# Rotary turn of the differential queries and keys: from GpSimd to VectorE and transfers issued by SyncE

## Chip, cores and metric

The kernel runs on one core of a Trainium2 chip. The metric is the device time of one execution in microseconds; a profiled execution gives the rows below. TensorE multiplies matrices, VectorE and ScalarE work on elements, GpSimd does the rest, and SyncE issues the transfers. The profile calls them PE (with PEld for its weight loads), DVE, ACT, POOL and SP.

## What is computed

Two transformer blocks of two layers each, one sequence of 256 tokens, 1024 features, fp32. The change touches the second block. A layer of it projects the input x into three branches and merges them:

```python
z, xbc, dt_raw, dq, dk, dv, dg, cq, cg, gl = jnp.split(proj, splits, axis=-1)
y_ssd = _ssd_branch(z, xbc, ...)      # scan over tokens; then y * silu(z), rms norm
q = _apply_rope(dq, cos, sin)         # each head: 2 x 64 features
k = _apply_rope(dk, cos, sin)
...                                   # differential attention over q, k, v, then norm
y_cross = ...                         # attention to a memory
merged = g0 * (y_ssd @ w0) + g1 * (y_diff @ w1) + g2 * (y_cross @ w2)

def _apply_rope(t, cos, sin):
    t1, t2 = t[..., :32], t[..., 32:]
    return concat([t1 * c - t2 * s, t1 * s + t2 * c])
```

With features on the partitions the turn is `t * cosT + swapped(t) * sinT`, where `swapped` exchanges the 32-row halves of every 64 partitions and the sign lies in `sinT`. [...]

## The kernel before

A product of 256 tokens with 256 output features is a "gemm" (`gemm`, line 320): two pieces of 24 matmuls each, into one PSUM bank `g`. For each piece the weights `w` arrive in 512 KB transfers (L280, up to 8 pieces ahead) and are split in two parts, `wh` by ScalarE (L290) and `wl` by VectorE (L292), up to 4 pieces ahead. Pieces wait in a queue `e.q`; `fill(n)` runs n of them between steps of other work, `need(tag)` runs the queue until no piece of that tag is left. A scheduler then sets the order of instructions on every engine from the order of the code, with the splits given priority.

In a layer of the second block the scan goes over 32 heads, two at a time. For each head (`scan_a`) GpSimd spreads a row over the partitions (L1456, PARTITION_BROADCAST into `E`) and cuts it twice (L1460, AFFINE_SELECT), ScalarE takes six exponentials (L1455), VectorE adds and multiplies (L1463, L1464). `scan_b` then multiplies the pair's `E` with the inputs (`yps`) and adds the result into `xsT` (L1476). `E` has four buffers. Between heads `fill` runs 48 pieces, and 48 are queued when the scan begins: the last 16 are those of `dq` and `dk`, four gemms each.

At the end of each of these eight gemms ScalarE copies the bank into `dq` or `dk` (L1418). After every second one `rotate` turns 128x1024 on GpSimd: four transfers issued by GpSimd into `sw` (L1404, L1405), then three operations (L1408 to L1410). Behind the scan come the eight `z` gemms (VectorE multiplies into `xsT`, `split` gives `ysh` and `ysl`), the gate and product of the state space branch (`b0`, 24 pieces), and between their pieces the differential attention `diff`, head by head, which begins with the products `ds` of `dq` and `dk`.

Of the kernel before, what the change touches and what calls it, by code (L numbers as in the profile page):

```python
# [16 lines left out]
P = 128  # L17
S = 256
# [6 lines left out]
# ------------------------------------------------------------------ host layout  # L25
# small parameters and constants that are loaded together: name, columns
# [8 lines left out]
# Column groups (256 wide) of the first block's w_in.  # L35
# [15 lines left out]
def _chunks(v, n=P):  # L51
    """[..., C] -> [n, ..., C / n] (feature on the partition)."""
    v = np.asarray(v)
    lead = v.shape[:-1]
    r = v.reshape(lead + (v.shape[-1] // n, n))
    return np.ascontiguousarray(np.moveaxis(r, -1, 0)).reshape(n, -1)


def _pack_in(w):
    """[L, K, G * 256] -> [L, G, 128, K / 128 * 256]: 256 output columns at a time."""  # L60
    L, K, M = w.shape
    r = w.reshape(L, K // P, P, M // 256, 256).transpose(0, 3, 2, 1, 4)
    return np.ascontiguousarray(r).reshape(L, M // 256, P, -1)


def _pack_rows(w):
    """[L, G * 256, 1024] -> [L, G, 128, 2 * 1024]: 256 contraction rows at a time."""
    L, K, M = w.shape
    r = w.reshape(L, K // 256, 2, P, M).transpose(0, 1, 3, 2, 4)
    return np.ascontiguousarray(r).reshape(L, K // 256, P, -1)  # L70
# [8 lines left out]
def _constants():  # L79
# [5 lines left out]
    dist = (t[:, None] - t[None, :]).astype(np.float32)  # [q, k]  # L85
# [16 lines left out]
    # compressed branch: bias and mask, [128, 2 (q tile), 4, 16]  # L102
# [7 lines left out]
    # rotary tables of the latent mixer: rows 64..95 of a head  # L110
# [14 lines left out]
    # second block: frequencies  # L125
# [8 lines left out]
def _pack(inp):  # L134
# [4 lines left out]
    # [L, 6 (modulation), 4, 128, 2 * 1024]: 256 contraction rows at a time  # L139
# [8 lines left out]
    # [L, 4, 128, 2 * 1024]: twice half of the contraction, two groups of 256 columns; twice a quarter, all groups  # L148
# [20 lines left out]
    # second block  # L169
# [35 lines left out]
# ------------------------------------------------------------------ device  # L205
NW, NS = 8, 4  # buffers of the streamed weights: raw, split
AHEAD_W, AHEAD_S = 8, 4  # pieces fetched, split ahead
SPLIT_FIRST, NORM_FIRST = 100, 200  # steps by which splits and norms go ahead in the schedule
NU = 11  # units of [128, 2048] words
# [6 lines left out]
class Emit:  # L216
# [50 lines left out]
    # ---- streamed weights, in the order of their use and in pieces of 1024 columns: the raw  # L267
    # tile, then its rounded part and the remainder
# [35 lines left out]
    # ---- queue of matrix products that fill the tensor engine's waits  # L304
# [15 lines left out]
    def gemm(self, tag, keys, act, evac, tok=False, half=None):  # L320
        """Queue a product of 256 tokens and 256 output features (the contraction in steps of
        1024, one key each; with half, half of a step); act(i) gives the two parts of the
        activations of step i. Features on the partitions, or tokens (tok)."""
# [37 lines left out]
    def token_sum(self, st, c, p, first, last):  # L361
        """st[token, tile] += sum over the partitions of c [p, 256]"""
# [3 lines left out]
    def spread(self, col):  # L366
        """[128 tokens, 2] -> PSUM [128, 256], the same on all partitions"""
# [19 lines left out]
    def fold(self, pool, box, pair):  # L387
        """box[0] += a pair of chunks [128, 512]"""
# [7 lines left out]
    def fold_sum(self, box):  # L396
        """the sums over features, [token, tile]"""
# [28 lines left out]
# ------------------------------------------------------------------ memory keys and values  # L426
# [9 lines left out]
def mem_gemm(e, l, g, hl, mk, mv, tag="mem"):  # L436
    """Group g of the layer's memory keys (0..3, features on the partitions) and values (4..7)."""
# [7 lines left out]
# ------------------------------------------------------------------ first block  # L445
def block1(e, ctx, mem0):
# [7 lines left out]
    # order of the streamed weights  # L454
    ada = lambda l, s: [("w_ada", l, s, n) for n in range(4)] if l < DEPTH else []
    zorder = (0, 1, 2, 3, 5, 4, 6, 7, 8)
    # modulations (shift, scale, gate; twice a layer) in the mixers, at the second norm, in the
    # products after it and at the next layer's norm
# [6 lines left out]
    MEM = 6  # memory groups at the start; the others come after the block  # L465
# [19 lines left out]
    # silu(c), replicated over 32 columns  # L485
# [13 lines left out]
    def ada_step(l, s, n):  # L499
        """a step of one of the layer's modulations: four column blocks side by side"""  # L500
# [21 lines left out]
    def ada_pool(l, s, n):  # L522
        """the same step on GpSimd: weighted rows, still to be summed over the partitions"""
# [31 lines left out]
    # the first modulations arrive at the memory's pace: its keys and values go between  # L555
# [29 lines left out]
    class Attend:  # L585
        """q(h), k(h): [d, 256] on partitions; v(h, t): [128, 64]; o: two PSUM tiles."""
# [4 lines left out]
        def scores(self):  # L591
            q, k, bs, par = self.q, self.k, self.bs, self.par
            # heads whose keys lie on different row tiles go to different banks
# [75 lines left out]
    def mixers(l, ah, al, oh, ol, ev_x):  # L669
# [70 lines left out]
        # compressed keys and values  # L740
# [5 lines left out]
        def compress(i):  # L746
# [5 lines left out]
            # element (lp, b) is token 16 b + 2 lp (+ 1 on the upper half)  # L752
# [33 lines left out]
        # latent attention: norms, queries, keys, values  # L786
# [27 lines left out]
        # rotary part, rows 64..95  # L814
# [20 lines left out]
        # gates of the sparse mixer  # L835
# [7 lines left out]
        # sliding window: heads 0, 2 | 1, 3 share a chunk of queries  # L843
# [16 lines left out]
        # sparse mixer: compressed, selected and window branches into one output  # L860
# [73 lines left out]
    for l in range(DEPTH):  # L934
# [40 lines left out]
        def down(g):  # L975
            """two pieces; the last one finishes one pair of chunks after the other"""
# [68 lines left out]
# ------------------------------------------------------------------ second block  # L1045
def block2(e, ctx, xh, xl, mk, mv, out):
# [18 lines left out]
    # halves, so that silu(u) = (tanh(u / 2) + 1) * (u / 2)  # L1065
# [5 lines left out]
    # rotary tables from the positions: reduced to [-pi, pi]  # L1071
# [36 lines left out]
    def silu2(ps_, dst):  # L1108
        """dst = 2 silu(ps_)"""
# [4 lines left out]
    # order of the streamed weights  # L1114
# [21 lines left out]
    def soft(scs, scale):  # L1136
        """scs: PSUM [128, 2, 256] -> exponentials, reciprocals of their sums [128, 2]"""
# [10 lines left out]
    def turn(src, dst, eng):  # L1148
        """src: [128 q, 2 (tile), 256 k] -> dst [128 k, 2 (tile), 256 q]"""
# [6 lines left out]
    def finish(l, xh, xl, act, G):  # L1156
        """the last product and layer norm, with the tokens on the partitions"""
# [33 lines left out]
        # the last groups one half of the tokens after the other  # L1191
# [14 lines left out]
    for l in range(DEPTH):  # L1206
# [17 lines left out]
        # ---------------- memory cross attention  # L1224
        def conv(ps, ch, dst):
            """channels ch, ch + 1 (128 each)"""
# [12 lines left out]
        bcT = v3(e.unit("bcT"), 8)  # B of the four groups, then C  # L1239
# [44 lines left out]
        # step sizes, [64 (direction, head), 256]  # L1284
# [7 lines left out]
        LO = e.t(cp, [P, S], "LO")  # rows 0..63: running sums in a chunk; 64..127: rest of the chunk  # L1292
        Lc = e.t(cp, [64, S], "Lc")  # the running sums alone
        bias = e.t(cp, [P, 2, P], "ltok")  # per token: log of the step and minus the running sum, or rest of the chunk

        def steps():
# [26 lines left out]
            # log of the step sizes, added to the exponents  # L1323
# [28 lines left out]
        # ---------------- queue of what the scan leaves room for  # L1352
# [49 lines left out]
        def rotate(tq, sw, hs):  # L1402
            for p0 in range(0, P, 64):
                nc.gpsimd.dma_start(sw[p0 : p0 + 32, hs, :], tq[p0 + 32 : p0 + 64, hs, :])  # L1404
                nc.gpsimd.dma_start(sw[p0 + 32 : p0 + 64, hs, :], tq[p0 : p0 + 32, hs, :])  # L1405
            sb_ = sinT.unsqueeze(1).to_broadcast([P, 4, S])
            cb_ = cosT.unsqueeze(1).to_broadcast([P, 4, S])
            nc.gpsimd.tensor_tensor(sw[:, hs, :], sw[:, hs, :], sb_, ALU.mult)  # L1408
            nc.gpsimd.tensor_tensor(tq[:, hs, :], tq[:, hs, :], cb_, ALU.mult)
            nc.gpsimd.tensor_tensor(tq[:, hs, :], tq[:, hs, :], sw[:, hs, :], ALU.add)  # L1410

        for key in ("dq", "dk"):
            for g in range(4):
                def ev_d(ps, g=g, key=key):
                    if g == 0:
                        dqk[key] = v3(e.unit(key), KC)
                        dqk["sw"] = v3(e.unit("sw"), KC)
                    nc.scalar.copy(dqk[key][:, 2 * g : 2 * g + 2, :], v3(ps, 2))  # L1418
                    if g % 2 == 1:
                        rotate(dqk[key], dqk["sw"], slice(4 * (g // 2), 4 * (g // 2) + 4))  # L1420
                e.gemm("dqk", G(key, g), act, ev_d)

        # ---------------- scan, one head at a time; two heads share a chunk of features
        state = {}

        def scan_a(h):
            g = h // 8
            if h % 8 == 0:
                e.need(f"xs{g}")
                if g % 2 == 0:  # L1430
                    state["xst"] = e.unit("xst")  # [token, (group, tile, channel)]
# [15 lines left out]
            # running sums of both directions on all partitions: [source chunk, token], then the other direction  # L1447
            # inside a chunk; GpSimd copies them and cuts off what the direction does not reach
# [18 lines left out]
        def scan_b(h, Es, xst):  # L1467
            """the pair of heads h, h + 1"""
# [8 lines left out]

        pend, Es = None, []
        for h in range(32):
            E, xst = scan_a(h)  # L1480
            Es.append(E)
            if pend:
                scan_b(*pend)
                pend = None
# [3 lines left out]
        scan_b(*pend)  # L1488
        e.need("dqk")

        # ---------------- gate of the state space branch, its norm
        ysh = [v3(e.unit("ysh", F32R), KC) for _ in range(2)]
        ysl = [v3(e.unit("ysl", F32R), KC) for _ in range(2)]
        stb, rsb = [], []
        for g in range(8):
            def ev_z(ps, g=g):
# [170 lines left out]
```

## Time and profile before

| | us |
|---|---|
| three runs | 1917.38, 1905.91, 1910.5 (median 1910.5) |
| span of the profiled execution | 1906.2 |
| PE busy in it | 1805.6 (95%) |
| DVE busy | 1339.7 (70%) |
| ACT busy | 1015.5 (53%) |
| POOL busy | 427.1 (22%) |

The profiled execution is given by its span alone; that span lies 4.3 us below the median of the runs and 0.3 us above the lowest. A busy share is an average over stages: what a stage is worth is read from its own stretch.

### The profile page before, as it was taken

The page shows a single profiled execution, that of the slowest core. Times are in us where ns is not written, and L with a number is a line of the kernel's source. Part 1 is how long each engine was busy: PE and PEld are TensorE (multiplying, and loading weights), DVE is VectorE, ACT ScalarE, POOL GpSimd, SP SyncE. Part 2 cuts the span into 40 slices and gives each one's busy share as a digit, 9 for nine tenths or more (in the row PEclk, how much of TensorE's full clock was granted, in tenths as well). Part 3 has the DMA queues.
Part 4 walks back from the last instruction along what each step waited for, and adds up shares of the span by engine and source line. Part 5 has one row for each costly group of instructions (what it writes and reads, how often), then busy time and mean ns, then how long its engine had stood idle before and what let it go on. Part 6 is the DMA issues. An engine that isn't in the chain of part 4 may idle for free.

```text
span 1906.2 us, 37110 instructions
## 1 busy us (share of the span) xinstructions
PE 1805.6 (95%) x14800; PEld 1703.3 (89%) x14800; DVE 1339.7 (70%) x2164; ACT 1015.5 (53%) x1882; POOL 427.1 (22%) x347
## 2 busy tenths in 40 slices
PE   7999999999989999999997699999999999499998
PEld 6878899978879999999996599999999998399998
DVE  4576766756778556887973897667787884597566
ACT  3454444434554445567874375454556774365542
POOL 0000463600028000013543601100002543601100
PEclk9999999999989999999999799999999999799999
DMA  9873876776357555443443353455543444245451
GB/s 333 320 262 128 296 250 207 243 274 221 129 204 256 179 188 182 167 147 138 155 164 103 122 175 135 174 203 177 181 166 136 135 164 144 88 162 181 145 177 67
DMA packets 96685, 346.86 MB, mean 182 GB/s; under 512 B 11776, under 2 KB 12928, under 8 KB 96256
## 3 DMA queue, kind: packets, MB, share of 16 engines
q1 hardware_dynamic: 94976, 340.30, 51.0%
q0 software_dynamic: 1536, 4.20, 0.8%
q8 instruction: 116, 1.90, 0.4%
q14 instruction: 57, 0.47, 0.1%
HBM read 339.01 MB, written 1.05 MB: 178 GB/s over the span
## 4 chain that ended last, share of the span: by engine, by line
PE 83%; DVE 6%; ACT 3%; issue 3%; DMA 2%; POOL 2%; POOLq 0%; SPq 0%; DVEq 0%; ACTq 0%
PE g L318 62%; PE acc L318 9%; DVE wl L292 2%; PE yps L318 1%; ACT wh L290 1%; PE ada L318 1%; PE sc L318 1%; PE o L318 1%; ACT E L1455 1%; DMA w<-w_mem 1%; PE do L318 1%; PE ds L318 1%; PE xo L318 1%; PE xs L318 1%; PE tw L1153 1%
## 5 line engine op out<-in xcount | busy, mean ns | idle before, releaser
L292 DVE TENSOR_TENSOR wl<-w,wh 128x1024 fp32r<-128x1024 f32 x518 | 686.3, 1329 | 358.0 <-ACT wh L290 356.4
L290 ACT CAST wh<-w 128x1024 fp32r<-128x1024 f32 x518 | 540.5, 1048 | 511.6 <-PE g L318 327.6
L318 PE MATMUL g<-xh,wh 128*128 128x256 f32 x1664 | 477.7, 287 | 3.3 <-ACT wh L290 2.7
L318 PE MATMUL g<-xh,wl 128*128 128x256 f32 x1664 | 473.2, 284 | 3.0 <-DVE wl L292 3.0
L318 PE MATMUL g<-xl,wh 128*128 128x256 f32 x1664 | 473.8, 285 | 0.0
L318 PEld LDWEIGHTS g<-xh,wh 128*128 128x128 f32 x1664 | 320.7, 193 | 15.9 <-issue 5.9
L318 PEld LDWEIGHTS g<-xh,wl 128*128 128x128 f32 x1664 | 321.0, 193 | 4.0 <-DVE wl L292 3.8
L318 PEld LDWEIGHTS g<-xl,wh 128*128 128x128 f32 x1664 | 321.1, 193 | 2.1 <-issue 2.0
L318 PE MATMUL g<-ah,wh 128*128 128x256 f32 x736 | 210.7, 289 | 3.1 <-ACT ah L552 3.1
L318 PE MATMUL g<-al,wh 128*128 128x256 f32 x736 | 211.0, 287 | 1.5 <-DVE al L553 1.5
L318 PE MATMUL g<-ah,wl 128*128 128x256 f32 x736 | 211.3, 288 | 0.7 <-DVE wl L292 0.7
L358 POOL TENSOR_TENSOR rsy<-rv,mhalf 128x2 f32<-128x2 f32 (+1 forms) x14 | 13.4, 957 | 882.2 <-DVE rv L375 778.1
L1455 ACT ACTIVATE E<-E,ltok 128x128 f32<-128x128 f32 x384 | 123.8, 395 | 116.1 <-POOL E L1456 65.7
L318 PE MATMUL acc<-pt,wh 128*128 128x256 f32 x1024 | 183.4, 280 | 1.0 <-DVE pt L971 1.0
L1456 POOL PARTITION_BROADCAST E<-rows x64 | 92.3, 1502 | 383.6 <-PE tw L1153 157.8
L318 PEld LDWEIGHTS acc<-pt,wh 128*128 128x128 f32 x1024 | 156.9, 188 | 1.6 <-DVE pt L971 1.2
L318 PEld LDWEIGHTS g<-ah,wh 128*128 128x128 f32 x736 | 142.5, 195 | 6.8 <-issue 3.5
L318 PEld LDWEIGHTS g<-al,wh 128*128 128x128 f32 x736 | 143.3, 195 | 3.4 <-DVE al L553 2.8
L318 PEld LDWEIGHTS g<-ah,wl 128*128 128x128 f32 x736 | 143.1, 194 | 1.3 <-DVE wl L292 1.1
L318 PE MATMUL acc<-pt,wl 128*128 128x256 f32 x512 | 142.3, 279 | 0.0
L531 POOL TENSOR_SCALAR sb<-w,ca 128x1024 f32<-128x1024 f32 x24 | 92.0, 3834 | 62.4 <-PE ada L318 32.8
L318 PEld LDWEIGHTS acc<-pt,wl 128*128 128x128 f32 x512 | 96.2, 188 | 0.0
(389 smaller groups left out, 3630.2 us busy)
## 6 DMA issues: line engine op xcount, KB each, us to landing
w<-w_ada SPq DMA_DIRECT2D x96, 512.0 KB
w<-w_up SPq DMA_DIRECT2D x64, 512.0 KB
w<-w_down SPq DMA_DIRECT2D x64, 512.0 KB
w<-w_br SPq DMA_DIRECT2D x64, 512.0 KB
w<-w_gl SPq DMA_DIRECT2D x48, 512.0 KB
w<-w_in SPq DMA_DIRECT2D x36, 512.0 KB
w<-w_mem SPq DMA_DIRECT2D x32, 512.0 KB
w<-w_out SPq DMA_DIRECT2D x32, 512.0 KB
```

What stands on the lines that cost most here:

```text
L290: nc.scalar.copy(wh, w)
L292: nc.vector.tensor_tensor(wl, w, wh.bitcast(F32), ALU.subtract)
L318: self.nc.tensor.matmul(o, l, r, start=start, stop=stop)
L358: self.nc.gpsimd.tensor_tensor(y, v, self.mhalf[:, 0:cols], ALU.pow)
L531: nc.gpsimd.tensor_scalar(dst, w, ca[:, 2 * n + i : 2 * n + i + 1], None, ALU.mult)
L1153: nc.tensor.transpose(tps[:, kt * S + t * P : kt * S + (t + 1) * P], src[:, t, kt * P : (kt + 1) * P], e.ident)
L1455: ex = lambda o, s, r: nc.scalar.activation(o, o, AF.Exp, bias=bias[:, s, r : r + 1])
L1456: nc.gpsimd.partition_broadcast(E, state["rows"][32 * (h % 4) : 32 * (h % 4) + 1, :])
```

## The change

The turn of `dq` and `dk` is made gemm by gemm (128x512) by VectorE, from the PSUM bank; ScalarE's copy goes into a tile `raw` instead of `dq`, and four transfers issued by SyncE bring the exchanged halves into a tile `sw` of the ring `gt`. The unit `sw` of 128x2048 is gone. The `z` gemms are queued while the scan runs, behind `dq` and `dk`; their splits into `ysh` and `ysl`, and the norm, become nine entries of their own in the queue, behind `z` and ahead of `b0`. The comments that are dropped elsewhere do nothing.

```diff
-        def rotate(tq, sw, hs):
-            for p0 in range(0, P, 64):
-                nc.gpsimd.dma_start(sw[p0 : p0 + 32, hs, :], tq[p0 + 32 : p0 + 64, hs, :])
-                nc.gpsimd.dma_start(sw[p0 + 32 : p0 + 64, hs, :], tq[p0 : p0 + 32, hs, :])
-            sb_ = sinT.unsqueeze(1).to_broadcast([P, 4, S])
-            cb_ = cosT.unsqueeze(1).to_broadcast([P, 4, S])
-            nc.gpsimd.tensor_tensor(sw[:, hs, :], sw[:, hs, :], sb_, ALU.mult)
-            nc.gpsimd.tensor_tensor(tq[:, hs, :], tq[:, hs, :], cb_, ALU.mult)
-            nc.gpsimd.tensor_tensor(tq[:, hs, :], tq[:, hs, :], sw[:, hs, :], ALU.add)
-
         for key in ("dq", "dk"):
             for g in range(4):
                 def ev_d(ps, g=g, key=key):
                     if g == 0:
                         dqk[key] = v3(e.unit(key), KC)
-                        dqk["sw"] = v3(e.unit("sw"), KC)
-                    nc.scalar.copy(dqk[key][:, 2 * g : 2 * g + 2, :], v3(ps, 2))
-                    if g % 2 == 1:
-                        rotate(dqk[key], dqk["sw"], slice(4 * (g // 2), 4 * (g // 2) + 4))
+                    raw, sw = e.t(tp_, [P, 512], "cv", bufs=3), e.t(tp_, [P, 512], "gt", bufs=2)
+                    nc.scalar.copy(raw, ps)
+                    dst = dqk[key][:, 2 * g : 2 * g + 2, :]
+                    nc.vector.tensor_tensor(dst, v3(ps, 2), cosT.unsqueeze(1).to_broadcast([P, 2, S]), ALU.mult)
+                    for p0 in range(0, P, 64):
+                        nc.sync.dma_start(sw[p0 : p0 + 32, :], raw[p0 + 32 : p0 + 64, :])
+                        nc.sync.dma_start(sw[p0 + 32 : p0 + 64, :], raw[p0 : p0 + 32, :])
+                    nc.vector.tensor_tensor(v3(sw, 2), v3(sw, 2), sinT.unsqueeze(1).to_broadcast([P, 2, S]), ALU.mult)
+                    nc.vector.tensor_tensor(dst, dst, v3(sw, 2), ALU.add)
                 e.gemm("dqk", G(key, g), act, ev_d)
...
+        def z_gemm(g):
+            def ev_z(ps):
+                zs = e.t(tp_, [P, 512], "cv", bufs=3)
+                silu2(ps, zs)
+                c0 = 2 * g % 8
+                y = flat(xsT[g // 4][:, c0 : c0 + 2, :])
+                nc.vector.scalar_tensor_tensor(y, zs, 0.5, y, ALU.mult, ALU.mult)
+                e.square(tp_, stb, y)
+            e.gemm("z", G("z", g), act, ev_z)
...
             if pend:
                 scan_b(*pend)
+                if pend[0] % 4 == 2:
+                    z_gemm(pend[0] // 4)
                 pend = None
...
         scan_b(*pend)
+        z_gemm(7)
         e.need("dqk")
...
+        def split_y(g):
+            for ch in (2 * g, 2 * g + 1):
+                e.split(ysh[ch // 8][:, ch % 8, :], ysl[ch // 8][:, ch % 8, :], xsT[ch // 8][:, ch % 8, :], ssd_w[:, l * 16 + ch : l * 16 + ch + 1])
+
+        def norm_y():
+            bc = e.rstd(tp_, e.fold_sum(stb), 2048, LN_EPS)
+            rsb.append(e.t(cp, [P, S], "rsb"))
+            nc.vector.tensor_copy(rsb[0], bc[:, 0:S])
+
+        e.add("zn", norm_y)
         for g in range(8):
-            def ev_z(ps, g=g):
...
+            e.add("zn", lambda g=g: split_y(g))
         branch(0, lambda i: (ysh[i], ysl[i]), "b0")
```

GpSimd's order at the last heads of layer 0's scan, before (a row that is only `ISA` switches what GpSimd has loaded; `ISA E<-rows` is the broadcast):

```order
L1456 ISA
L1456 ISA E_12098<-rows_11955 128x768
L1456 ISA E_12151<-rows_11955 128x768
L1460 AFFINE_SELECT E_12098<-E_12098 128x2x128
L1408 ISA
L1408 TENSOR_TENSOR sw_11575<-sw_11575,sinT_8574 128x1024
L1409 TENSOR_TENSOR dq_11574<-dq_11574,cosT_8573 128x1024
L1460 AFFINE_SELECT E_12098<-E_12098 128x256
```

The same place in the change (lines there are numbered 4 lower):

```order
L1452 ISA E_12129<-rows_11984 128x768
L1452 ISA E_12191<-rows_11984 128x768
L1456 AFFINE_SELECT E_12129<-E_12129 128x2x128
L1456 AFFINE_SELECT E_12129<-E_12129 128x256
L1456 AFFINE_SELECT E_12191<-E_12191 128x2x128
L1456 AFFINE_SELECT E_12191<-E_12191 128x256
L358 ISA
L358 TENSOR_TENSOR rsy_13042<-rv_13040,mhalf_74 128x2
```

The turn's rows and the switches between heads are gone from GpSimd; one switch is left, behind the last select.

VectorE's order in the change, around the turn of the third and fourth `dq` gemm (L1411 the multiplication by cosT, L1415 by sinT, L1416 the sum):

```order
L1411 TENSOR_TENSOR dq_11574<-g_11716,cosT_8573 128x512 [waits Activation_49]
L1472 SCALAR_TENSOR_TENSOR xsT_8578<-xsT_8578,pack_1302_8564,yps_11850 128x256 [waits PE_49]
L292 TENSOR_TENSOR wl_11858<-w_11636,wh_11856 128x1024 [waits DMAHW1_49,Activation_49]
L1415 TENSOR_TENSOR gt_11794<-gt_11794,sinT_8574 128x512 [waits DMAHW2_49,DMAHW3_49,DMAHW1_49,DMAHW0_49]
L1416 TENSOR_TENSOR dq_11574<-dq_11574,gt_11794 128x512 [waits DVE_49]
L292 TENSOR_TENSOR wl_11915<-w_11721,wh_11913 128x1024 [waits PE_49,Activation_49]
L1411 TENSOR_TENSOR dq_11574<-g_11803,cosT_8573 128x512 [waits Activation_49]
```

Between the two multiplications stand two other rows here; the second one waits for four transfers, and the split `wl` of a later piece stands behind it.

TensorE's order behind the last `yps` of that scan, before:

```order
L318 MATMUL yps_12236<-E_12098,xst_11097 64x256
L318 MATMUL yps_12236<-E_12151,xst_11097 64x256
L318 MATMUL g_12286<-xh_8526,wh_12120 128x256
L318 MATMUL g_12286<-xl_8527,wh_12120 128x256
L318 MATMUL g_12286<-xh_8526,wl_12122 128x256
```

and in the change:

```order
L318 MATMUL yps_12278<-E_12129,xst_11097 64x256
L318 MATMUL yps_12278<-E_12191,xst_11097 64x256
L318 MATMUL ds_12301<-dk_11973,dq_11574 128x256
L318 MATMUL ds_12302<-dk_11973,dq_11574 128x256
L318 MATMUL ds_12301<-dk_11973,dq_11574 128x256
L318 MATMUL ds_12302<-dk_11973,dq_11574 128x256
L318 MATMUL g_12328<-xh_8526,wh_12151 128x256
```

The first `z` product still stands behind the last `yps`; the first head's `ds`, which before came 112 matmuls later, now stands ahead of it.

## Rows read from the trace of the kernel before

**Rows 1.** The page: span, and PE busy and granted clock in 40 slices.
```profile
span 1906.2 us, 37110 instructions
...
PE   7999999999989999999997699999999999499998
...
PEclk9999999999989999999999799999999999799999
```

**Rows 2.** Waits of PE, whole run: total us, times, longest.
```profile
PE yps L318 <- DVE E L1464: 48.8, 12, 12.4
```

**Rows 3.** Stretches: busy us (instructions) per engine, then granted clock, DMA share, GB/s.
```profile
core 0: us, PE busy (x) PEld busy (x) DVE busy (x) ACT busy (x) POOL busy (x), PEclk, DMA share, GB/s
940.00:1000.00 60.00, 60.00 (x487) 55.80 (x486) 47.52 (x73) 43.99 (x97) 25.66 (x35) 1.00 0.49 171
1000.00:1080.00 80.00, 53.38 (x378) 46.67 (x377) 38.88 (x29) 28.44 (x58) 46.77 (x42) 0.83 0.33 104
1080.00:1150.00 70.00, 68.56 (x567) 66.24 (x566) 64.07 (x117) 46.99 (x109) 2.00 (x2) 1.00 0.48 166
...
1600.00:1680.00 80.00, 52.80 (x376) 46.12 (x375) 43.04 (x34) 26.90 (x53) 45.68 (x39) 0.83 0.32 105
```

**Rows 4.** The chain that ended last, 1000 to 1085 us: start, us, what.
```profile
1036.71 5.47 issue
...
1044.73 6.70 issue
...
1076.04 7.43 DVE wl L292 x3
```

**Rows 5.** Waits of POOL from 1000 to 1080 us: total us, times, longest.
```profile
POOL E L1456 <- issue: 11.6, 2, 5.8
POOL dq L1410 <- issue: 7.5, 1, 7.5
POOL sw L1408 <- DMA w<-w_z: 6.9, 1, 6.9
POOL sw L1408 <- issue: 6.8, 1, 6.8
```

**Rows 6.** Line L1408, whole run: duration ns min/median/max.
```profile
L1408 POOLq MODIFY_POOL_CONFIG  x8: 2/10/12, 1001.9 to 1635.4; - x8
L1408 POOL TENSOR_TENSOR sw<-sw,sinT x8: 2328/2820/3255, 1008.8 to 1662.6; 128x1024 f32<-128x1024 f32 x8
```

**Rows 7.** POOL in order of time, before the first turn: start, us.
```profile
986.49 3.45 POOL L1456 PARTITION_BROADCAST E<-rows  x2 [4.87 <-PE yps L318]
990.02 1.48 POOL L1460 TENSOR_SCALAR_AFFINE_SELECT E<-E 128x256 f32<-128x256 f32 x4
```

**Rows 8.** Groups of DVE from 940 to 1000 us: busy us, mean ns.
```profile
L292 DVE TENSOR_TENSOR wl<-w,wh 128x1024 fp32r<-128x1024 f32 x19 | 24.1, 1273 | 10.8 <-ACT wh L290 10.7
L1464 DVE TENSOR_TENSOR E<-E,gm 128x512 f32<-128x512 f32 x10 | 6.8, 685 | 0.1
L1463 DVE TENSOR_TENSOR E<-E 128x256 f32<-128x256 f32 x10 | 4.2, 419 | 0.7 <-ACT E L1455 0.7
```

**Rows 9.** Groups of DVE from 1000 to 1080 us.
```profile
L292 DVE TENSOR_TENSOR wl<-w,wh 128x1024 fp32r<-128x1024 f32 x13 | 25.6, 1984 | 16.6 <-ACT wh L290 16.6
L1464 DVE TENSOR_TENSOR E<-E,gm 128x512 f32<-128x512 f32 x6 | 10.0, 1663 | 0.2
L1463 DVE TENSOR_TENSOR E<-E 128x256 f32<-128x256 f32 x6 | 4.7, 778 | 22.6 <-ACT E L1455 22.6
L1476 DVE SCALAR_TENSOR_TENSOR xsT<-xsT,pack,yps 128x256 f32<-128x256 f32 x4 | 1.9, 474 | 1.7 <-PE yps L318 1.7
```

**Rows 10.** Transfers of tile dq, tile dk, and SP's small ones: landing; issue ns.
```profile
DMA to landing us min/median/max: 2.4/3.6/6.1
...
DMA to landing us min/median/max: 2.2/2.7/2.8
...
L1452 SPq DMA_DIRECT2D rows<-Lc x64: 497/503/652, 796.7 to 1573.0; - x64
```

**Rows 11.** Waits of SP's queue from 1000 to 1080 us.
```profile
SPq L280 <- DVE wl L292: 76.3, 12, 22.7
```

More of the change, by code (lines that the diff above doesn't have):

```diff
@@ L1476, in scan_b @@
             nc.vector.scalar_tensor_tensor(y, y, d_skip[:, l * 16 + ch : l * 16 + ch + 1], yps[:, 0:S], ALU.mult, ALU.add)
+        stb, rsb = [], []
+        def z_gemm(g):
[7 more added lines that the diff above has]
+            e.gemm("z", G("z", g), act, ev_z)
         pend, Es = None, []
@@ L1493, in block2 @@
         ysl = [v3(e.unit("ysl", F32R), KC) for _ in range(2)]
-        stb, rsb = [], []
-        for g in range(8):
-            def ev_z(ps, g=g):
-                zs = e.t(tp_, [P, 512], "cv", bufs=3)
-                silu2(ps, zs)
-                c0 = 2 * g % 8
-                y = flat(xsT[g // 4][:, c0 : c0 + 2, :])
-                nc.vector.scalar_tensor_tensor(y, zs, 0.5, y, ALU.mult, ALU.mult)
-                for c in range(2):
-                    ch = 2 * g + c
-                    e.split(ysh[ch // 8][:, ch % 8, :], ysl[ch // 8][:, ch % 8, :], xsT[ch // 8][:, ch % 8, :], ssd_w[:, l * 16 + ch : l * 16 + ch + 1])
-                e.square(tp_, stb, y)
-                if g == 7:
-                    bc = e.rstd(tp_, e.fold_sum(stb), 2048, LN_EPS)
-                    rsb.append(e.t(cp, [P, S], "rsb"))
-                    nc.vector.tensor_copy(rsb[0], bc[:, 0:S])
-            e.gemm("z", G("z", g), act, ev_z)
+        def split_y(g):
[6 more added lines that the diff above has]
+        e.add("zn", norm_y)
+        for g in range(8):
+            e.add("zn", lambda g=g: split_y(g))
         branch(0, lambda i: (ysh[i], ysl[i]), "b0")
@@ L1580, in block2 @@
             pass
-        e.need("z")
+        e.need("zn")
         e.fill(4)
```

## Prediction

> **What bounds the kernel now.** The page comes first [rows 1]: PE is busy in nearly every slice, so only the thin places can give time back. In the second block there are two: slices 22 and 23, about 1001 to 1096 us, and slice 35, about 1620 to 1668 us, one place in each layer, and there the granted clock is below full too. Next, the waits of PE [rows 2]: the greatest of the run is `yps`, the scan's product, waiting for VectorE's L1464, 48.8 us in twelve waits. Third, the stretches [rows 3]. From 940 to 1000 us, in the scan but before the turn, PE issues 487 matmuls in 60 us, 8.12 per us. From 1000 to 1080 us, where the turn runs, it issues 378 in 80 us, at a mean granted clock of 0.83, between its levels of 1.2 and 2.4 GHz. From 1080 to 1150 us it is back at 567 in 70 us, 8.10 per us. Layer 1 repeats it: 376 in 80 us. At 8.12 per us the 378 take 46.6 us and the 376 take 46.3 us, so the two stretches lose 33.4 and 33.7 us, **67.1 us** together. Lost clock is in that number, since it counts matmuls and not busy time.
>
> Fourth, why. The chain of work through the stretch has long pieces that the profile calls issue, 5.47 and 6.70 us among them [rows 4]. The waits of POOL say where they stand [rows 5]: twice 5.8 us ahead of a broadcast, 7.5 us ahead of the turn's sum, 6.9 and 6.8 us ahead of its first multiplication; 32.8 us in one layer in which POOL waited for nothing that matters. The turn's line holds a MODIFY_POOL_CONFIG beside each multiplication [rows 6], and in GpSimd's order a bare `ISA` stands where it passes from broadcast and select to the turn. The records last some ns, the silence behind them 6 to 7 us. Before the turn begins broadcast and select follow each other with no such silence, 3.45 us for two broadcasts and 1.48 us for four selects, and POOL waits for PE [rows 7]. So the scan does not lack GpSimd time: it pays for alternating with the turn, and then for the turn's own operations of 2.3 to 3.3 us each [rows 6]. While these run VectorE slows as well: the same `wl` split has a mean of 1273 ns before and 1984 ns in the stretch, L1464 685 against 1663, L1463 419 against 778 [rows 8, 9], and the chain closes with three splits in 7.43 us [rows 4].
>
> **What is removed.** All of the turn's GpSimd rows, and with them every switch between heads; the one left stands behind the last select, with `rsy` far behind it, and is hidden by the pieces of `z`. If nothing is late in its place the scan's end keeps the pace of 940 to 1000 us: −67.1 us.
>
> **What is added, on VectorE.** Three operations of 128x512 for each of eight gemms and two layers, 48. L1464 has that shape: 685 ns, 16.4 us a layer. From rows 9 the stretch's own work at the undisturbed means is 13 × 1.273 + 6 × 0.685 + 6 × 0.419 + 4 × 0.474 = 25.1 us. With the turn it is 41.5 us in 46.6 us of PE: VectorE fits, with 5.1 us to spare. Behind it, 1080 to 1150 us, VectorE is busy 64.07 of 70 us with PE at full pace [rows 3], another 5.9 us.
>
> The new wait costs more thought. The multiplication by `sinT` waits in line for four transfers. The first may go when ScalarE's copy ends, four issues take 4 × 0.50 = 2.0 us [rows 10], and landing takes 2.7 us if it is like `dk`'s, 3.6 us like `dq`'s, with bounds of 2.2 and 6.1 us [rows 10]; those were 128 KB transfers of GpSimd's, these are 64 KB of SyncE's, which no row shows. I take 2.7, since half the bytes go. Against these 4.7 us stand the multiplication by `cosT` (0.69) and what the order puts between the two, from one row to five, about 1.9 us on the mean: VectorE stands still 2.1 us, and 17 us over eight turns, 12 us more than it has to spare. Queued behind it are `wl` splits, for which PE waits, and the scan's L1463 and L1464. But a wait of this kind shrinks when VectorE is late: the transfers have started from ScalarE's side, and splits are made some three pieces ahead, which at 24 matmuls a piece and 8.12 per us is 8.9 us of cover. So one delay of about 2 us may shift VectorE once, and later turns find their data landed. Between 0 and 12 us a layer I take 3, near the low end because of that cover: **+6 us**. Without the cover it would be +24 us. A landing of 2.2 us makes the wait 1.6 us, within the same choice; one of 6.1 us makes it 5.5 us, 44 us a layer, 39 more than VectorE has to spare, of which the cover and the next stretch would have to take what they can: the upper bound below.
>
> The Trainium skill (DMA: Bandwidth & Descriptors, Anatomy of one DMA) fits a transfer issued by GpSimd with 2.0 us plus its bytes at 436 GB/s, an estimate of 2.15 us for 64 KB. By that the wait would be about 1.6 us a turn, and the total the same within 1 us; the trace's medians of 2.7 and 3.6 us lie above the fit, and decide.
>
> **What is moved, at nothing.** SyncE issues 64 more transfers, each some 0.5 us, 16 us a layer. In the stretch SP's queue waits 76.3 of 80 us for a buffer of the weights [rows 11], so it has the time; behind a swap that waits for ScalarE stand weight transfers that run eight pieces, over 20 us, ahead of PE. ScalarE copies as often as before. `z`: 48 fills meet 48 queued pieces, so no `z` product enters the scan, and PE's order shows the first one behind the last `yps` still. The nine new entries take 9 of `diff`'s 32 fills, but the scheduler has put splits right behind each `z` again; their work is the same 16 splits. If it were not hidden, `b0` would start late by the last split pair, under 2 us. `ds` of the first head, ahead by 112 matmuls, needs only the first `dq` and `dk` gemms, turned long before: no gain is counted.
>
> **Sum.** 1906.2 − 67.1 + 6 = 1845 us for a profiled execution. The median of the runs is 4.3 us above that span, so **1850 us**, 3.2% less.
>
> **Rivals.** (a) *VectorE becomes the bound.* Landings at 3.6 to 6.1 us, a wait of 3.0 to 5.5 us a turn, 24 to 44 us a layer, of which VectorE's spare 5.1 and the next stretch's 5.9 take 11: 13 to 33 us lost a layer if the cover takes nothing, half of it if it takes half. Roughly 7 to 25 us a layer, 1857 to 1893 us. For it: VectorE has 89% of the stretch filled before any wait. Against it: the cover.
>
> (b) *Slower: the swaps stand behind weights.* Before, the turn's transfers had GpSimd's queue; now they share SyncE's with 512 KB weight transfers, which at the stretch's own pace of 171 GB/s [rows 3] last 3.1 us each. The place is L1415. With no cover it decides where a turn costs (33.5 + 5.1 + 5.9) / 8 = 5.6 us, that is, at a landing of 6.2 us, one or two weights ahead of it; with the 8.9 us of cover used up first, not before 15 us. At two weights ahead, 2.7 + 6.2 = 8.9 us, a wait of 8.3 us, 66 us a layer, 55 after the spare: 1906.2 + 2 × (55 − 33.5) + 4.3, about 1953 us without cover. Against it: the transfers fill only 0.49 of the DMA engines' time in the full-pace stretch [rows 3], so seldom do two weights wait there.
>
> The Trainium skill (DMA: Bandwidth & Descriptors, Queues, rings and completion order) says that a DMA engine takes turns between the queue rows that have work, and drains each in order. By that rule the old swaps passed between weights and the new ones wait behind them, which is this rival's mechanism; no row here shows a swap on SyncE's queue.
>
> (c) *The silences stay.* If they come from something other than the alternation, only the turn's operations go: about five of them lie on the chain, 5 × 2.3 = 12 us a layer, 1906.2 − 24 + 4.3 = 1887 us, or no gain where the scan's next link fills it. Against it: rows 7.
>
> **How the numbers follow.** The forecast's own case, 0 to 6 us lost a layer, runs from 1843 to 1856 us and has 0.68. (a) has 0.19, (b) 0.04, (c) 0.06, half of it a gain; 0.03 is left for more than the 67 us coming back, since VectorE also loses its slow splits behind 1080 us. The range of 8 in 10 goes from 1838 (a low run, 5 us below the forecast's best) to 1880, in the upper half of (a). Two versions of this kernel can be told apart at about 0.5%, 9.6 us: faster by more than that is the forecast, nearly all of (a) and half of (c), 0.92; within it 0.04; slower 0.04.
>
> **What the new profile would show.** Right: PE near 8.1 matmuls per us through both stretches and clock 1.00 there; no MODIFY_POOL_CONFIG between the broadcasts of a scan; `wl` at 1.27 us throughout; `yps` gone from the head of PE's waits. L1415's idle time before it, and what releases it, is the measure of the term of 6 us: some us in total, in the first turns of each layer. Wrong: L1415 with over 30 us of idle time, followed by PE waiting for `wl` (a, b); or POOL silences of 6 to 7 us between heads still (c).

## Result and the profile after

The change runs in 1838.8 us (median of four runs, 1836.3 to 1842.4) against 1909.1 us before: ratio 0.9629, interval 0.9607 to 0.9651, 3.7% less. The forecast was 1850 us in a range of 1838 to 1880.

The page of the changed kernel; the two thin places of [rows 1] are filled, and the clock no longer falls there:

```profile
span 1837.0 us, 37186 instructions
...
PE   7999999999998999999999999999999999999998
...
PEclk9999999999998999999999999999999999999999
```

Stretches of the changed kernel, columns as in [rows 3]:

```profile
1000.00:1080.00 80.00, 80.00 (x655) 75.77 (x655) 72.90 (x124) 52.39 (x114) 17.23 (x18) 1.00 0.57 177
1046.00:1110.00 64.00, 64.00 (x527) 61.79 (x526) 59.85 (x116) 47.06 (x109) 0.74 (x1) 1.00 0.47 155
1610.00:1680.00 70.00, 70.00 (x584) 68.48 (x583) 60.84 (x113) 48.77 (x110) 7.66 (x8) 1.00 0.53 176
```

The same 80 us that held 378 matmuls now hold 655, 8.19 per us, and TensorE is never idle in them. GpSimd's busy time there falls from 46.77 to 17.23 us. VectorE's rises from 38.88 to 72.90.

The greatest wait of [rows 2] is all but gone (PE's waits, changed kernel, whole run; L1460 is the former L1464):

```profile
PE g L318 <- ACT wh L290: 9.6, 1, 9.6
...
PE yps L318 <- DVE E L1460: 1.0, 2, 0.5
```

GpSimd in order of time, changed kernel (start, us):

```profile
1009.78 3.26 POOL L1452 PARTITION_BROADCAST E<-rows  x2 [4.85 <-PE yps L318]
1013.11 3.39 POOL L1456 TENSOR_SCALAR_AFFINE_SELECT E<-E 128x256 f32<-128x256 f32 x4
1019.77 3.16 POOL L1452 PARTITION_BROADCAST E<-rows  x2 [3.27 <-DVE E L1459]
```

Broadcast and select follow each other as in [rows 7], and GpSimd waits for TensorE or VectorE: it is ahead again. The silences of [rows 5] have no successor.

VectorE's groups from 1000 to 1080 us, changed kernel (busy us, mean ns, idle time before them and what ended it):

```profile
L292 DVE TENSOR_TENSOR wl<-w,wh 128x1024 fp32r<-128x1024 f32 x24 | 30.2, 1259 | 0.7 <-ACT wh L290 0.7
...
L1415 DVE TENSOR_TENSOR gt<-gt,sinT 128x512 f32<-128x512 f32 x7 | 5.7, 811 | 6.2 <-DMA gt<-cv 6.2
```

The split `wl` is back from 1984 to 1259 ns. The new wait exists, and it is VectorE's: 6.2 us here. With 72.90 us busy and 0.7 us of waiting for ScalarE that makes 79.8 of 80 us: VectorE is nearly full, yet TensorE waits for it nowhere in these 80 us. The line L1415 over the whole run:

```profile
L1415 DVE TENSOR_TENSOR gt<-gt,sinT x16: 681/693/1396, 998.7 to 1602.0; 128x512 f32<-128x512 f32 x16
its engine sat idle before it (us, times) until:
  DMA gt<-cv: 10.1, 11
```

Eleven of sixteen turns wait, 10.1 us together.

### The profile page after: what moved, and what is told of

Its sections match the earlier page's. It is cut to its first block, busy times and chain, and to the rows that moved or that the text cites. A ratio compares the mean times of both kernels' runs of the same rounds, so it can differ in the third digit from the quotient of the medians.

```text
span 1837.0 us, 37186 instructions
## 1 busy us (share of the span) xinstructions
PE 1791.6 (98%) x14800; PEld 1696.7 (92%) x14800; DVE 1334.8 (73%) x2212; ACT 1017.1 (55%) x1882; POOL 358.9 (20%) x291
## 4 chain that ended last, share of the span: by engine, by line
PE 90%; DVE 3%; ACT 2%; DMA 2%; issue 1%; POOL 0%; POOLq 0%; SPq 0%; DVEq 0%; ACTq 0%
PE g L318 68%; PE acc L318 10%; PE yps L318 2%; DVE wl L292 1%; PE sc L318 1%; PE ada L318 1%; PE ds L318 1%; PE o L318 1%; DMA w<-w_ada 1%; ACT wh L290 1%; PE do L318 1%; PE xs L318 1%; PE xo L318 1%; DMA w<-w_up 1%; PE tw L1153 1%
## 5 line engine op out<-in xcount | busy, mean ns | idle before, releaser
L292 DVE TENSOR_TENSOR wl<-w,wh 128x1024 fp32r<-128x1024 f32 x518 | 664.3, 1285 | 337.7 <-ACT wh L290 335.5
L1452 POOL PARTITION_BROADCAST E<-rows x64 | 96.6, 1571 | 389.0 <-PE tw L1153 157.7
```

Of the source, the lines that this page charges most:

```text
L292: nc.vector.tensor_tensor(wl, w, wh.bitcast(F32), ALU.subtract)
L1452: nc.gpsimd.partition_broadcast(E, state["rows"][32 * (h % 4) : 32 * (h % 4) + 1, :])
```

## The experiments

Theory A: the loss was mostly the silences in which GpSimd passes from broadcast to product and back. The rivals: GpSimd's products themselves, by their time and by holding up VectorE (B), or something in the new order of `z`. In the edits, lines of the kernel that is changed stand without a sign where they only show the place.

| run | median us (range) | ratio to before (interval) |
|---|---|---|
| turn only | 1838.7 (1838.2 to 1843.9) | 0.9630 (0.9609 to 0.9652) |
| `z` only | 1908.4 (1903.6 to 1911.9) | 0.9991 (0.9978 to 1.0005) |
| tiny switch | 1864.2 (1860.1 to 1867.1) | 0.9754 (0.9734 to 0.9773) |
| two hops | 1843.9 (1841.3 to 1846.7) | 0.9649 (0.9632 to 0.9667) |
| late turn | 1892.4 (1890.4 to 1897.1) | 0.9909 (0.9888 to 0.9931) |
| select turn | 1854.9 (1854.1 to 1860.8) | 0.9715 (0.9696 to 0.9734) |
| late products | 1878.4 (1876.3 to 1881.1) | 0.9832 (0.9816 to 0.9847) |
| GpSimd's queue | 1838.7 (1837.0 to 1839.9) | 0.9623 (0.9608 to 0.9637) |
| select switch | 1892.0 (1887.0 to 1902.5) | 0.9917 (0.9886 to 0.9947) |
| late selects | 1864.8 (1859.9 to 1867.9) | 0.9758 (0.9731 to 0.9785) |

**The halves of the change.** "Turn only" is the kernel before with the change's `ev_d` and without `rotate`. "`z` only" is the change with `rotate` and the old `ev_d` put back.

```diff
 # z only
-                    raw, sw = ...
...
-                    nc.vector.tensor_tensor(dst, dst, v3(sw, 2), ALU.add)
+                    nc.scalar.copy(dqk[key][:, 2 * g : 2 * g + 2, :], v3(ps, 2))
+                    if g % 2 == 1:
+                        rotate(dqk[key], dqk["sw"], slice(4 * (g // 2), 4 * (g // 2) + 4))
```

> The turn alone is moved to VectorE and SyncE; the z products, their splits and the norm stay as before. Theory (the whole gain comes from taking the turn off GpSimd): within 5 us of the change, 1834 to 1844 us. Rival (the new order of z and its splits brings part of it): 1850 us or more.

> The z products join the queue in the scan and their splits become entries of their own; the turn stays on GpSimd. Theory: within 5 us of the kernel before, 1904 to 1914 us. Rival (z fills the stalls of the scan): 1895 us or less.

The turn alone gives all of it, the `z` products and split entries nothing that can be measured.

**One switch put back.** The change, with a product of two columns on GpSimd at every second gemm:

```diff
                     nc.scalar.copy(raw, ps)
+                    if g % 2 == 1:
+                        tiny = e.t(tp_, [P, 2], "tiny", bufs=2)
+                        nc.gpsimd.tensor_tensor(tiny, raw[:, 0:2], e.mhalf[:, 0:2], ALU.mult)
```

> The change, plus one GpSimd product of 128x2 (an unused tile) after every second gemm of dq and dk, four a layer: the alternation without the work. Its order on GpSimd has four switches inside each scan, where the kernel before had five. Theory A (the 6 to 7 us silences at each switch cost the time): four silences make 26 us a layer, of which the scan absorbs what the five silences and 12 us of operations of the kernel before lost of their 45 us, about 12 us; 14 to 26 us a layer, 1867 to 1891 us, with silences of 6 to 7 us in GpSimd's time line. Theory B (the turn's own operations on GpSimd, and VectorE slowed by them, cost it): 1837 to 1843 us.

GpSimd in order of time, "tiny switch":

```profile
1005.37 0.60 POOL L1412 TENSOR_TENSOR tiny<-cv,mhalf 128x2 f32<-128x2 f32 x1 [6.87 <-PE yps L318]
...
1013.84 1.98 POOL L1455 PARTITION_BROADCAST E<-rows  x2 [7.86 <-issue]
...
1031.88 0.20 POOL L1412 TENSOR_TENSOR tiny<-cv,mhalf 128x2 f32<-128x2 f32 x1 [7.91 <-DVE wl L292]
...
1038.44 2.48 POOL L1455 PARTITION_BROADCAST E<-rows  x2 [6.36 <-issue]
```

Work of 0.2 to 0.6 us has a gap of 6.4 to 7.9 us on either side (the first one may hold a wait for `yps` too: in the change GpSimd waits 6.92 us for it at that place), and 25.4 us of the run are lost. So the alternation costs by itself, even where next to nothing is computed; B without it falls. The loss is a little under A's band. The four gaps of this layer sum to 29.0 us, of which 12.7 us a layer came into the time, so more was absorbed than the 12 us that A allowed for. That fits the 15.1 us that the change's GpSimd waits for TensorE and VectorE from 1000 to 1080 us, since a gap in the place of such a wait costs nothing; it isn't shown gap by gap.

**The cover.** The change, with each swap landing in another tile first and four more transfers bringing it on:

```diff
-                        nc.sync.dma_start(sw[p0 : p0 + 32, :], raw[p0 + 32 : p0 + 64, :])
-                        nc.sync.dma_start(sw[p0 + 32 : p0 + 64, :], raw[p0 : p0 + 32, :])
...
+                        nc.sync.dma_start(mid[p0 : p0 + 32, :], raw[p0 + 32 : p0 + 64, :])
+                        nc.sync.dma_start(mid[p0 + 32 : p0 + 64, :], raw[p0 : p0 + 32, :])
+                    for p0 in range(0, P, 32):
+                        nc.sync.dma_start(sw[p0 : p0 + 32, :], mid[p0 : p0 + 32, :])
```

> The change, with the exchanged halves landing in a second tile first and four more transfers bringing them into the ring: the multiplication by sinT waits some 4 to 5 us longer, at each of 16 turns. Theory (VectorE may be late by up to the 8.9 us by which the splits run ahead, at no cost to PE): 1837 to 1845 us, with VectorE's idle time before L1415's like grown to 30 us or more. Rival (each wait goes straight into the time, since VectorE is nearly full there): 64 to 80 us of waits less some 20 us of spare, 1880 us or more.

The time met the expectation, the reason did not. The line of the multiplication by `sinT`, "two hops", and a wait of TensorE (whole run):

```profile
L1419 DVE TENSOR_TENSOR gt<-gt,sinT x16: 674/690/1286, 1000.1 to 1608.7; 128x512 f32<-128x512 f32 x16
...
  DMA gt<-mid: 15.2, 5
```

```profile
PE do L318 <- DVE pt L1154: 3.8, 2, 2.1
```

The scheduler put more rows between the two multiplications, so that only five turns waited, 15.2 us instead of the 30 or more expected. The idle time grew by 5.1 us and the median time by 5.1 us (the spans of the two profiled executions lie 2.5 us apart), and products `do` of the differential attention now wait 3.8 us for VectorE, which they don't in the change. That fits a VectorE with little room to spare, but the order moved too: it is no clean test of the cover. "GpSimd's queue", below, is a cleaner one.

**The turn behind the scan.** The kernel before, with `rotate` taken out of `ev_d`:

```diff
         e.need("dqk")
+        sws = {key: v3(e.unit("sw"), KC) for key in ("dq", "dk")}
+        for i in range(2):
+            for key in ("dq", "dk"):
+                rotate(dqk[key], sws[key], slice(4 * i, 4 * i + 4))
```

> The kernel before with its turn on GpSimd, all four turns of a layer put behind the scan: the same operations and transfers, one switch instead of five. Theory A (alternating inside the scan is the greater part): the scan keeps 8.1 matmuls per us to its end, z covers the turn, and VectorE slowed by it costs some us a layer: 1840 to 1865 us. Theory B (the operations themselves cost the greater part, wherever they stand): 1885 us or more.

Theory A failed here. "Late turn": the stretch behind the scan (columns as in [rows 3]), GpSimd's order of time, the split `wl` from 1040 to 1100 us, and a wait of TensorE (whole run):

```profile
1040.00:1100.00 60.00, 43.09 (x303) 39.54 (x301) 52.67 (x48) 23.51 (x49) 26.38 (x16) 0.83 0.37 122
```

```profile
1030.46 3.29 POOL L1408 TENSOR_TENSOR sw<-sw,sinT 128x1024 f32<-128x1024 f32 x1 [7.40 <-issue]
...
1038.26 0.94 POOL L1457 TENSOR_SCALAR_AFFINE_SELECT E<-E 128x256 f32<-128x256 f32 x2
```

```profile
L292 DVE TENSOR_TENSOR wl<-w,wh 128x1024 fp32r<-128x1024 f32 x12 | 36.3, 3036 | 6.5 <-ACT wh L290 6.5
```

```profile
PE g L318 <- DVE wl L292: 23.6, 7, 11.3
```

Two things: the scheduler still put a product, with its silence, ahead of the last selects; and behind the scan VectorE is busy 52.67 of 60 us with only 48 instructions, its splits at 3036 ns on the mean (1216 in the change behind its scan), while TensorE waits for them. The second was new, and the next runs are for it.

**Products without switches to pay.** "Late products" is the change with twelve products of 128x1024, whose results nothing uses, behind the scan. "Late selects" has thirty selects of that size there instead, which read one input.

```diff
         e.need("dqk")
+        dead, full = e.unit("dead"), state["xst"]
+        for i in range(12):
+            nc.gpsimd.tensor_tensor(dead[:, 0:1024], full[:, 0:1024], full[:, 1024:2048] if i else flat(xsT[1][:, 4:8, :]), ALU.mult)
```

> The change, plus twelve unused products of 128x1024 on GpSimd behind each scan, which nothing waits for but the last z gemm: only VectorE's slowing by GpSimd is added, some 30 us a layer. If that slowing is part of what the change won: L292 at 1.9 us or more there and 5 to 12 us a layer, 1849 to 1863 us. If splits ahead absorb it: 1837 to 1844 us.

> The change, plus thirty unused AFFINE_SELECTs of 128x1024 on GpSimd behind each scan, 31 us or more of one-input work where the run with twelve products had 34 us of two-input work. If only two-input products shut VectorE out: 1837 to 1846 us, L292 near 1.27 us there. If any GpSimd instruction does, for as long as it lasts: 1850 to 1880 us, L292 at 1.6 us or more.

The products cost 39.6 us, far above both expectations, though GpSimd has nothing else to do there. The selects cost 25.9 us, in the band of "any GpSimd instruction", though they keep GpSimd busy for longer (44.4 us in the first of the two layers against 34.1 us). VectorE's groups behind the scan, first the change (1044 to 1078 us):

```profile
L292 DVE TENSOR_TENSOR wl<-w,wh 128x1024 fp32r<-128x1024 f32 x9 | 10.9, 1216 | 0.7 <-ACT wh L290 0.7
L1140 DVE TENSOR_REDUCE sm<-ds 128x2 f32<-128x512 f32 x6 | 3.9, 682 | 0.0
...
L1547 DVE TENSOR_SCALAR E<-E,sd 128x256 f32<-128x256 f32 x6 | 1.8, 348 | 0.0
...
L1145 DVE RECIPROCAL sd<-sd 128x2 f32<-128x2 f32 x6 | 0.9, 154 | 0.0
```

then "late products" in the same stretch:

```profile
L292 DVE TENSOR_TENSOR wl<-w,wh 128x1024 fp32r<-128x1024 f32 x4 | 10.1, 2519 | 0.0
L1550 DVE TENSOR_SCALAR E<-E,sd 128x256 f32<-128x256 f32 x2 | 4.9, 2498 | 0.0
...
L1140 DVE TENSOR_REDUCE sm<-ds 128x2 f32<-128x512 f32 x4 | 2.6, 676 | 0.0
...
L1145 DVE RECIPROCAL sd<-sd 128x2 f32<-128x2 f32 x2 | 0.3, 152 | 0.0
```

and "late selects":

```profile
L292 DVE TENSOR_TENSOR wl<-w,wh 128x1024 fp32r<-128x1024 f32 x7 | 12.1, 1726 | 0.3 <-ACT wh L290 0.3
...
L1550 DVE TENSOR_SCALAR E<-E,sd 128x256 f32<-128x256 f32 x4 | 3.9, 1004 | 0.0
...
L1140 DVE TENSOR_REDUCE sm<-ds 128x2 f32<-128x512 f32 x4 | 2.6, 676 | 0.0
```

The reduction of `ds`, which reads PSUM, and the reciprocal keep their time; the split takes twice its time beside the products, and the multiplication of `E` (`TENSOR_SCALAR`) seven times. That this is a wait for GpSimd's instruction shows in the smallest one. In "late products" VectorE's order of time has

```profile
1044.27 1.76 DVE L1534 SCALAR_TENSOR_TENSOR nlam<-ls 128x1 f32<-128x1 f32 x1
1045.96 1.27 DVE L1140 TENSOR_REDUCE sm<-ds 128x2 f32<-128x512 f32 x2
```

where the change takes 0.15 us for the same 128 elements, and GpSimd's product in "late products" is

```profile
1042.71 3.31 POOL L1504 TENSOR_TENSOR dead<-xst,xsT 128x1024 f32<-128x1024 f32 x1 [17.20 <-DVE xsT L1472]
```

The product ends at 1046.02, VectorE's instruction at 1046.03.

The Trainium skill (SBUF — State Buffer, Who interferes with whom) says that GpSimd shares a pair of ports with VectorE as an exclusive lock for the whole instruction: a GpSimd instruction that reads SBUF contends with VectorE instructions of two SBUF inputs, and GpSimd with copies and `tensor_scalar` in their two-port modes, while one SBUF input outside those modes, or a `tensor_reduce`, is free. The rows above agree (the mode of the `TENSOR_SCALAR` no row names): two-input splits 1216 to 2519 ns, `TENSOR_SCALAR` 348 to 2498, reduction 682 to 676, reciprocal 154 to 152.

**Selects in the turn's place.** "Select turn" is the kernel before with the turn's three products replaced by five selects of 128x1024, so the turn itself is left out: no switches, GpSimd still busy. "Select switch" adds two products of two columns per turn, so that GpSimd passes back and forth as before.

```diff
-            nc.gpsimd.tensor_tensor(sw[:, hs, :], sw[:, hs, :], sb_, ALU.mult)
-            nc.gpsimd.tensor_tensor(tq[:, hs, :], tq[:, hs, :], cb_, ALU.mult)
-            nc.gpsimd.tensor_tensor(tq[:, hs, :], tq[:, hs, :], sw[:, hs, :], ALU.add)
+            sel = lambda o, i: nc.gpsimd.affine_select(out=o, in_=i, ...)
+            two(sw)   # select switch only: o[:, hs, 0:2] times o[:, hs, 2:4]
+            for i in range(2):
+                sel(sw[:, hs, :], sw[:, hs, :])
+            for i in range(2):
+                sel(tq[:, hs, :], tq[:, hs, :])
+            two(tq)   # select switch only
+            sel(tq[:, hs, :], sw[:, hs, :])
```

> The kernel before, with each turn's three products and sums on GpSimd replaced by five AFFINE_SELECTs of 128x1024 that copy (the turn itself is left out): GpSimd is as busy at the same places and behind the same transfers, and never switches. Theory A (the switches are the greater part): 1840 to 1865 us. Theory B (GpSimd's time and the waits for the transfers in its queue are): 1885 us or more.

> The kernel of the run with copying selects, plus one product of 128x8 on GpSimd where each turn's first multiplication and its sum stood: GpSimd's order has the kernel before's five switches inside the scan again, and its time, but its long operations are selects (the turn is left out). Theory C (what is left to the kernel before is VectorE shut out by GpSimd's long two-input products): the switches add 16 to 40 us to 1855 us, 1871 to 1895 us. Theory A (switches and GpSimd's time are all of it): 1903 us or more.

The stretch of the turn, "select turn", whole and in two parts, then "select switch":

```profile
1000.00:1060.00 60.00, 55.05 (x430) 50.68 (x429) 44.00 (x44) 32.65 (x65) 46.88 (x51) 0.94 0.59 185
1000.00:1050.00 50.00, 49.90 (x407) 46.35 (x405) 38.17 (x37) 30.36 (x62) 40.61 (x43) 1.00 0.60 190
1050.00:1060.00 10.00, 5.16 (x23) 4.33 (x24) 5.83 (x7) 2.29 (x4) 6.27 (x9) 0.66 0.54 161
```

```profile
1000.00:1060.00 60.00, 39.93 (x280) 36.82 (x279) 24.67 (x26) 23.04 (x51) 25.63 (x37) 0.80 0.30 95
```

A wait of TensorE, "select turn" (whole run):

```profile
PE ds L318 <- POOL dk L1406: 10.0, 2, 5.1
```

GpSimd in order of time, "select switch":

```profile
1018.89 1.98 POOL L1460 PARTITION_BROADCAST E<-rows  x2 [5.89 <-PE g L318]
...
1028.12 0.19 POOL L1407 TENSOR_TENSOR dq<-dq 128x8 f32<-128x8 f32 x1 [7.25 <-issue]
1028.28 1.49 POOL L1464 TENSOR_SCALAR_AFFINE_SELECT E<-E 128x256 f32<-128x256 f32 x4
```

With GpSimd busy 46.88 us in 60, more densely than in the kernel before, TensorE still gets 430 matmuls through; with five silences of 5.9 to 7.3 us (33.1 us in the layer) it gets 280. Each against its own runs of before, the steps are: before to select switch, the long products replaced by selects, 0.8% (0.5 to 1.1), some 16 us; select switch to select turn, the switches gone, 2.0%, some 39 us; select turn to the change, the selects gone too, 0.9%, some 16 us. Together the 70 us.

The last step is not a part of what the kernel before lost. In "select turn" TensorE keeps its pace up to 1050 us, 407 matmuls in 50 us, beside a GpSimd that is busy 40.61 of these 50 us and splits of 1476 ns. It loses at one place in each layer: GpSimd's turn ends late, `ds` stands close behind the scan in this order and waits 5 us for a result of the turn, and the granted clock is below full there, 0.66 on the mean from 1050 to 1060 us. In the kernel before the first `ds` starts at 1084.8 us and has no such wait. So inside this scan GpSimd's selects, and the VectorE that they slow, cost TensorE nothing, and the 39 us for the switches are what is left after a loss of some 15 us that came in with the order of "select turn".

**The queue that issues the swaps.** The change with `nc.gpsimd.dma_start` for the four swaps:

```diff
-                        nc.sync.dma_start(sw[p0 : p0 + 32, :], raw[p0 + 32 : p0 + 64, :])
+                        nc.gpsimd.dma_start(sw[p0 : p0 + 32, :], raw[p0 + 32 : p0 + 64, :])
```

> The change, with the swaps issued by GpSimd instead of SyncE: 32 issues a layer of some 0.5 us stand in GpSimd's order, each group waiting for ScalarE's copy with the next broadcasts behind it. Theory (GpSimd has about 5 us of every 10 to spare in the scan, and issuing a transfer makes no switch): 1837 to 1845 us. Rival (the broadcasts behind a waiting issue come late and the scan with them): 1853 us or more.

1838.7 us, the same as the change. "GpSimd's queue": the stretch of the turn, the multiplication by `sinT`, and GpSimd behind four issues that end at 1006.23 us:

```profile
1000.00:1080.00 80.00, 80.00 (x655) 75.46 (x654) 75.88 (x126) 55.16 (x123) 27.78 (x41) 1.00 0.55 178
```

```profile
L1415 DVE TENSOR_TENSOR gt<-gt,sinT x16: 676/682/1402, 999.1 to 1597.5; 128x512 f32<-128x512 f32 x16
its engine sat idle before it (us, times) until:
who waited for it (us, times):
```

```profile
1006.45 2.46 POOL L1452 PARTITION_BROADCAST E<-rows  x2 [0.23 <-PE yps L318]
```

A transfer issued by GpSimd brings no switch with it. No multiplication by `sinT` waits any more, where eleven did, VectorE gets more done in the 80 us (75.88 us against 72.90), and TensorE issues the same 655 matmuls. So the change's 10.1 us of waits cost TensorE nothing, and SyncE's weights don't hold the swaps up by anything that it sees.

No version beat the change; "turn only" and "GpSimd's queue" equal it.

## Why the prediction was right, step by step

The median lies 0.8 us above the range's lower end and below the forecast's own case of 1843 to 1856 us; the lowest of the four runs, 1836.3 us, lies outside the range. That it fell inside is in part luck.

**The lost stretch, −67.1 us.** Right. It was counted by matmuls, so it did not depend on how the loss divides. The profiled span went from 1906.2 to 1837.0 us, 69.2 us. The stretches with `diff` ran at 8.23 to 8.34 matmuls per us and not at 8.10. Counted by when the matmul of a given number starts, the two places gave back 35 and 36 us, and the change was 1.9 us behind when it reached the first of them.

**Why it was lost.** Right in kind: removing the switches alone, in their place, is worth some 39 us, the largest part, and some 54 by an estimate that leaves out the wait for `ds` that comes in with "select turn". But the sentence "it pays for alternating with the turn, and then for the turn's own operations" held two prices that the prediction left undivided, and the second is not GpSimd's time alone: VectorE is locked out while GpSimd reads. The prediction saw the slow splits and gave them no price. The long products, against selects in the same places, are worth some 16 us; how these divide between GpSimd's time and the lock, the runs don't separate. The 16 us between "select turn" and the change are the wait for `ds` and the lower clock after it, and no part of the loss before. That theory A failed when the turn moved behind the scan fits the lock, which went with it to a place where VectorE is nearly full (splits of 3036 ns, for which TensorE waits). The extra costs in the change (25 us for two round trips a scan, 40 and 26 for late products and selects) are prices at those places and don't add up to the 70.

**VectorE fits.** Right, and barely: 41.5 us in 46.6 was worked out; from 1000 to 1046 us it is busy 41.29 us. Over the 80 us it is busy 72.90 us, and most of the rest are its waits.

**The wait for the swaps, +6 us.** Wrong in size: TensorE lost nothing that its waits show; those for `wl` fell from 4.7 us to 1.7. The wait came out at 10.1 us on VectorE in both layers instead of 17 us in each if nothing shifted, and spread over the stretch, not in the first turns. Where VectorE waited, 2.1 to 5.9 us lay between the start of the fourth issue and the multiplication, 3.8 in the middle (a landing of 2.7 was taken), and an issue lasted 0.51 to 0.60 us (0.50 assumed). These would have made the waits longer; what made them shorter is that VectorE came late, as the prediction had argued. Its multiplication by `cosT` started 0.4 to 6.1 us after ScalarE's copy had ended, as here by 3.8 us:

```profile
1007.67 0.58 ACT L1409 COPY cv<-g 128x512 f32<-128x512 f32 x1
```

```profile
1012.05 0.68 DVE L1411 TENSOR_TENSOR dq<-g,cosT 128x512 f32<-128x512 f32 x1
```

This term makes 6 of the 11.2 us by which 1850 was too high. Another 2.5 us are the time around the span, 1.8 us (1838.8 against 1837.0) where 4.3 us were taken: that difference to the median held scatter between runs. The 69.2 us in place of 67.1 give 2.1 us, rounding the rest.

**At nothing.** Right for `z` (ratio 0.9991) and for SyncE's transfers (no difference when GpSimd issues them).

**Rivals.** (a) did not occur, though VectorE is nearly full: with its waits taken out ("GpSimd's queue") the time is the same. (b) did not occur. (c) is refuted: the silences come and go with a product of two columns. How long a wait the splits ahead would cover stays open, as "two hops" moved the order too.

## What to carry to other kernels

Count a GpSimd operation in three parts: its own time, what it costs to pass to it from another kind of operation and back, and the VectorE instructions that can't run beside it; the last two don't show in its own busy time. What each costs is read at its place: twenty selects of 128x1024 a layer cost TensorE nothing inside the scan, thirty behind it cost the run 25.9 us. A loss counted by the work that didn't get through (matmuls per us) stays right even when its division among causes is not yet known. When an edit fills the engine next to the bound, look at what the bound waits for, not at the fill: VectorE at 79.8 of 80 us, waits included, held TensorE up nowhere, and without the waits nothing was gained; five longer waits, 15.2 us in all, came with 5.1 us more. Whether the exchange needs transfers at all, no run tested: at L1320 of this kernel VectorE reads partitions 0 to 63 of `LO` and writes partitions 64 to 127, 0.28 us for 64x128.

## What the runs showed of the hardware that was not expected

- Between PARTITION_BROADCAST and TENSOR_TENSOR GpSimd is silent for 5.8 to 8.0 us in either direction, even for a product of two columns; AFFINE_SELECT (in "select switch" it starts 0.16 us after a product's start) and the issue of a transfer bring none. The Trainium skill (GPSIMD Engine Reference, Instruction dispatch) gives a first call to freshly loaded GpSimd code about 6 us, which no instruction in the profile shows; the shortest gaps here agree, the longest are 2 us longer (a wait for something else may be in them), and they are paid again at every return.
- A VectorE instruction on 128 elements took 1.76 us instead of 0.15, and ended with GpSimd's product. Selects, which have a single input, slow VectorE too (split 1726 ns instead of 1216).
